# Start addresses of TensorE's tiles set to one place modulo 256 bytes

## The chip, the cores and the metric

The kernel runs on one core of one Trainium2 chip. The metric is the device time of one execution in microseconds (us); lower is better. TensorE multiplies (its weight loads are listed apart), VectorE (DVE) and ScalarE (ACT) do the elementwise work, GpSimd (POOL) does a little of it and issues some DMAs, and SyncE (SP) issues nearly all loads from memory.

## The reference, cut to what matters

Two layers over 256 latent tokens and 256 context tokens of width 1024, all in float32. In the last layer the context tokens only give keys and values, so that most products there have 256 columns (tokens) and not 512.

```
for l in range(DEPTH):                                  # DEPTH = 2
    h  = modulate(rmsnorm(x,  norm1_g[l]), sh1, sc1)    # latent tokens
    hc = modulate(rmsnorm(xc, norm1_g[l]), csh1, csc1)  # context tokens
    p  = h @ w_in[l]                                    # 1024 x 4608
    ...                                                 # conv branch, attention, gates
    x  = x + g1 * gated_merge(p[..., QKV_END:], y_conv, y_attn, w_out[l])
    h2 = modulate(rmsnorm(x, norm2_g[l]), sh2, sc2)
    x  = x + g2 * conv_ffn(h2, w_up[l], ffn_dw[l], ffn_dw_b[l], w_down[l])
    if not last: ...                                    # the same for xc
return rmsnorm(x, final_norm_g)
```

## The kernel before, in words

Activations are held transposed: a tile has 128 channels on the partitions and the tokens along the free axis, latent tokens in columns 0 to 255, context tokens in 256 to 511. Weights come from memory in units of 128 x 1024 float32 (512 KB), each of which holds eight 128 x 128 blocks.

To keep float32 accuracy at TensorE's fast rate for the type float32r, every operand is split into a high and a low part. A weight unit lands in `raw`; ACT copies it to `whi` (L167) and DVE subtracts to get `wlo` (L168); for 33 units the low part is made by a DMA that adds (`wadded`). `raw`, `whi` and `wlo` have four buffers each. Activations are split in the same way into pairs: `h[0][k]` and `h[1][k]` for k = 0 to 7, `oh`/`ol`, `sh`/`sl`, `fh`/`fl`.

`mm3` (L185 to L188) is the core of the program: one product of a weight block and an activation tile is three matmuls, L186 (whi, high), L187 (whi, low) and L188 (wlo, high). Before each of them TensorE loads the 128 x 128 weight block that it keeps, while the tokens of the matmul before are streamed. `group` (L190) is eight such triples over k into one bank. In the value projection (L723) the roles are changed: the block of `h` is kept, and 512 columns of `whi` or `wlo` are streamed.

The sequence of instructions on each engine is the order in which the program's generators are written out (`slot()`, the list `side`, the rates `pace` and `rate`), as far as buffers being free allow it. SP and POOL are in-order queues as well: a DMA that waits for its buffer holds back the DMAs behind it.

Where the tiles start matters for this change. In the built program, with addresses inside a partition taken modulo 256 bytes:

- Each `h` tile is 2 * S + 2 = 514 columns, that is 2056 bytes, and takes 2080. So the eight tiles `h[0][0]` to `h[0][7]` start at 0, 32, 64, 96, 128, 160, 192 and 224, and `h[1][k]` at the same place as `h[0][k]`.
- `whi` and `wlo` start at 0 (the four units that open the last layer's FFN, in a pool of their own, at 128). A block inside a unit is 512 bytes further on, so it has the same place.
- `fh`/`fl` start at 128 in both layers; `oh`/`ol`/`sh`/`sl` at 64 in layer 0 and at 128 in layer 1.

Below, the *difference* of a step is the start of the block being loaded minus the start of the tile being streamed, modulo 256. In a group over `h` it runs through 0, 224, 192, 160, 128, 96, 64, 32 as k goes from 0 to 7. In a group over `fh` it is 128 all the time.

The two extra columns of `h` serve one place: before the last layer's FFN, unnormalised activations are written into the context half of the tiles `z` (`plain`, L996) and a shift into the two columns behind them (`plain_shift`, L1002), and the first four up units multiply columns 256 to 513 of these tiles (`RAW`, 258 columns, L1091).

Of the kernel before, what the change touches and what calls it, by code (L numbers as in the profile page):

```python
# [30 lines left out]
MASKED = -1.0e30  # L31
UW = 1024
LAT, CTX = slice(0, S), slice(S, 2 * S)
ROWS = S // GW
# [19 lines left out]
def trunk(ctx: ExitStack, tc: tile.TileContext, xt, cvec, crow, wall, wada, params, bias_t, rope_t, out):  # L54
# [34 lines left out]
    def add_side(gen):  # L89
        side.append(gen)  # L90
# [86 lines left out]
    def wunit(l, u, at=None, cuts=1):  # L177
        w, more = wparts(l, u, at, cuts)
        more()
        return w  # L180
# [18 lines left out]

    def wadded(l, u):  # L200

        r = raw_unit(wall[l, u])
        hi = wp.tile([P, UW], F32R, tag="whi", bufs=4, name=nm("whi"))
        lo = wp.tile([P, UW], F32R, tag="wlo", bufs=4, name=nm("wlo"))
# [5 lines left out]
    def unit8(l, u, at=None):  # L210
        w = wadded(l, u) if (l, u) in ADDED else wunit(l, u, at)
        return [cols(w, i) for i in range(KD)]
# [405 lines left out]
    for l in range(DEPTH):  # L618
# [3 lines left out]
        ALL = slice(0, T)  # L622

        with ExitStack() if last else start as e1a:
            ea = e1a.enter_context(tc.tile_pool(name=f"ea{l}", bufs=1)) if last else ea0
# [74 lines left out]
            with ExitStack() as e1b:  # L700
# [27 lines left out]
                if l == 0:  # L728
# [14 lines left out]
                    rv = wp.tile([P, UW], F32, tag="raw", bufs=4, name=nm("raw"))  # L743
                    wv = [wp.tile([P, UW], F32R, tag=t, bufs=4, name=nm(t)) for t in ("whi", "wlo")]
# [3 lines left out]
                    wg = [wp.tile([P, UW], F32R, tag=t, bufs=4, name=nm(t)) for t in ("whi", "wlo")]  # L748
                    with tc.issue_after(lastev[0].ins):
# [63 lines left out]
                else:  # L813
                    sp.dma_start(rope, rope_t)
                    pg0 = [psum("sc") for _ in range(2)]
                    for uu in range(2):
                        wg = wunit(l, U_GLU0 + uu)
# [91 lines left out]
            with ExitStack() as e1c:  # L909
# [57 lines left out]
                def branch(base, xh, xl):  # L967
                    for n in range(0, KD, 2):
                        w = (wadded if (l, base + n // 2) in ADDED else wunit)(l, base + n // 2)
                        for i in range(2):  # L970
                            yield n + i, group(psum(), [cols(w, 4 * i + k) for k in range(KC)], xh, xl, ALL)
# [21 lines left out]

                RAW = slice(S, 2 * S + 2)

                def plain(k):  # L996
                    hi, lo = z[0][k][:, CTX], z[1][k][:, CTX]
                    g = gains[l, 4][:, k, 0:1]
                    lastev[0] = act.activation(hi, x[k][:, LAT], AF.Identity, scale=g)
                    dve.scalar_tensor_tensor(lo, x[k][:, LAT], g, hi.bitcast(F32), ALU.mult, ALU.subtract)  # L1000

                def plain_shift(k):  # L1002
                    hi, lo = (z[i][k][:, 2 * S : 2 * S + 2] for i in range(2))
                    b = mod(l, 3, k, 0).to_broadcast([P, 2])
                    act.copy(hi, b)
                    dve.tensor_tensor(lo, b, hi.bitcast(F32), ALU.subtract)
# [15 lines left out]
                pace[0] = 0.3  # L1022
                held = [unit8(l, U_WO + n) for n in range(NB, KD)]
                for s in range(NS if held else 0):
# [14 lines left out]
        with ExitStack() as e2:  # L1039
# [42 lines left out]
            ups = [U_UP + t for i in range(KF) for t in (i, KF + i)]  # L1082
            first = [unit8(l, u, ef if last else None) for u in ups[:4]]
            pss = [psum("sc"), psum("sc"), psum(), psum()]
            if last:
# [3 lines left out]
                for k in range(KD):  # L1089
                    for w, ps in zip(first, pss):  # L1090
                        mm3(ps[:, : S + 2], w[k], h2[0][k][:, RAW], h2[1][k][:, RAW], k == 0, k == KD - 1)  # L1091
# [44 lines left out]
            for i in range(2, KF):  # L1136
                w = [unit8(l, ups[2 * i + t]) for t in range(2)]
                pa, pg = (group(psum(), w_, *h2, ALL) for w_ in w)
# [9 lines left out]
            else:  # L1148
                pace[0] = 0.3
                row = lambda: ef.tile([P, UW], F32, tag="row", bufs=2, name=nm("row"))  # L1150
                add_side(ada_dots(1, range(40, 48), [across(ef, 0)], row))
            for streams, ns in [((0, 1), range(NB)), *(((s,), range(NB, KD)) for s in range(NS))]:
                wu = None
                c = slice(streams[0] * S, (streams[-1] + 1) * S)
                for n in ns:
                    ps = psum()
                    for k in range(KF):
                        t = n * KF + k
                        if t % 8 == 0 or not wu:
                            wu = wunit(l, U_DN + t // 8)  # L1160
                        mm3(ps[:, c], cols(wu, t % 8), fh[k][:, c], fl[k][:, c], k == 0, k == KF - 1)
# [163 lines left out]
```

## Time and profile before

| | before |
|---|---|
| time, median of 3 runs | 1105.96 us (1105.14 to 1106.23) |
| span of the profiled execution | 1105.0 us |
| TensorE busy | 1092.9 us (99%), 6886 matmuls |
| VectorE busy | 895.7 us (81%) |
| ScalarE busy | 567.9 us (51%) |
| read from memory | 187.63 MB, 171 GB/s over the span |
| granted TensorE clock | 0.997 |

The span runs from the first to the last instruction; the runs' median is 0.96 us above it, and that is taken as what lies around the span. A matmul's duration in the profile reaches past the start of the next one, so that durations overlap and add up to more than the span; what one matmul costs is the time from its start to the start of the next, which is called a *step* here. A count of matmuls in a window includes those that are already running at its edge (about two).

### The profile page before, as it was taken

The page shows a single profiled execution, that of the slowest core. Times are in us where ns is not written, and L with a number is a line of the kernel's source. Part 1 is how long each engine was busy: PE and PEld are TensorE (multiplying, and loading weights), DVE is VectorE, ACT ScalarE, POOL GpSimd, SP SyncE. Part 2 cuts the span into 40 slices and gives each one's busy share as a digit, 9 for nine tenths or more (in the row PEclk, how much of TensorE's full clock was granted, in tenths as well). Part 3 has the DMA queues.
Part 4 walks back from the last instruction along what each step waited for, and adds up shares of the span by engine and source line. Part 5 has one row for each costly group of instructions (what it writes and reads, how often), then busy time and mean ns, then how long its engine had stood idle before and what let it go on. Part 6 is the DMA issues. An engine that isn't in the chain of part 4 may idle for free.

```text
span 1105.0 us, 18022 instructions
## 1 busy us (share of the span) xinstructions
PE 1092.9 (99%) x6886; PEld 949.4 (86%) x6886; DVE 895.7 (81%) x1630; ACT 567.9 (51%) x943; POOL 43.5 (4%) x59
## 2 busy tenths in 40 slices
PE   9999999999999999999999999999999999999997
PEld 6777777788889888888888888998889999999997
DVE  5568898889998788888897555789799888988773
ACT  4458767445334534343434223444676667666642
POOL 1111110011000000000000000000000000000000
PEclk9999999999999999999999999999999999999998
DMA  9888664978843445445567666566644484666781
GB/s 364 287 226 225 143 167 103 290 241 218 259 134 115 129 142 168 150 155 153 172 189 232 207 190 177 182 205 190 192 133 138 153 283 145 202 191 182 228 259 56
DMA packets 59510, 209.26 MB, mean 189 GB/s; under 512 B 7200, under 2 KB 7456, under 8 KB 59424
## 3 DMA queue, kind: packets, MB, share of 16 engines
q1 hardware_dynamic: 54384, 190.77, 53.8%
q0 software_dynamic: 4752, 17.30, 8.2%
q8 instruction: 54, 0.88, 0.3%
q14 instruction: 32, 0.26, 0.1%
q10 hardware_dynamic: 288, 0.04, 0.0%
HBM read 187.63 MB, written 1.05 MB: 171 GB/s over the span
## 4 chain that ended last, share of the span: by engine, by line
PE 89%; DVE 3%; ACT 3%; DMA 2%; issue 1%; SPq 1%; DVEq 0%; ACTq 0%
PE main L186 26%; PE main L188 26%; PE main L187 26%; PE main L723 4%; DMA raw<-in_wall 1%; SPq L715 1%; PE sc L186 1%; PE sc L187 1%; PE sc L188 1%; PE po L219 1%; PE po L564 1%; DVE cb L659 1%; PE sc L481 1%; ACT whi L167 1%; DVE wlo L168 0%
## 5 line engine op out<-in xcount | busy, mean ns | idle before, releaser
L186 PE MATMUL main<-h,whi 128*128 128x256 f32 (+1 forms) x1328 | 447.4, 337 | 0.0
L188 PE MATMUL main<-h,wlo 128*128 128x256 f32 (+1 forms) x1328 | 443.4, 335 | 1.1 <-DVE wlo L168 1.1
L187 PE MATMUL main<-h,whi 128*128 128x256 f32 (+1 forms) x1328 | 442.5, 334 | 0.1
L167 ACT CAST whi<-raw 128x1024 fp32r<-128x1024 f32 (+1 forms) x211 | 217.8, 1036 | 239.8 <-DMA raw<-in_wall 116.3
L168 DVE TENSOR_TENSOR wlo<-raw,whi 128x1024 fp32r<-128x1024 f32 (+1 forms) x211 | 252.7, 1205 | 88.6 <-ACT whi L167 83.5
L186 PEld LDWEIGHTS main<-h,whi 128*128 128x128 f32 x1328 | 249.6, 188 | 30.4 <-issue 2.2
L188 PEld LDWEIGHTS main<-h,wlo 128*128 128x128 f32 x1328 | 249.4, 188 | 29.8 <-DVE wlo L168 1.5
L187 PEld LDWEIGHTS main<-h,whi 128*128 128x128 f32 x1328 | 249.9, 188 | 28.5 <-DVE h L391 0.5
L659 DVE SCALAR_TENSOR_TENSOR cb<-u,par,cb 128x512 f32<-128x512 f32 (+1 forms) x240 | 144.0, 615 | 2.8
L186 PE MATMUL main<-fh,whi 128*128 128x256 f32 (+1 forms) x386 | 123.0, 319 | 0.0
L187 PE MATMUL main<-fl,whi 128*128 128x256 f32 (+1 forms) x386 | 122.9, 319 | 0.0
L188 PE MATMUL main<-fh,wlo 128*128 128x256 f32 (+1 forms) x386 | 122.9, 318 | 0.0
L293 DVE CUSTOM_DVE_ANT_0 t<-raw,sb,par 128x1024 bf16<-128x1024 f32 x72 | 91.4, 1277 | 0.3 <-ACT sb L273 0.3
L187 PEld LDWEIGHTS main<-fl,whi 128*128 128x128 f32 x386 | 72.7, 188 | 5.6
L188 PEld LDWEIGHTS main<-fh,wlo 128*128 128x128 f32 x386 | 72.7, 188 | 5.6
L186 PEld LDWEIGHTS main<-fh,whi 128*128 128x128 f32 x386 | 72.7, 188 | 5.5
L1052 ACT ACTIVATE t<-main,par 128x512 f32<-128x512 f32 (+1 forms) x82 | 50.8, 669 | 38.5 <-PE main L188 38.5
L293 DVE CUSTOM_DVE_ANT_0 t<-own,sb,par 128x1024 bf16<-128x1024 f32 x48 | 60.3, 1278 | 1.9 <-DMA own<-in_wada 1.9
L205 ACT CAST whi<-raw 128x1024 fp32r<-128x1024 f32 x33 | 34.6, 1049 | 51.0 <-PE main L187 43.8
L1053 DVE SCALAR_TENSOR_TENSOR t<-main,par,t 128x510 f32<-128x510 f32 (+1 forms) x82 | 47.5, 614 | 10.2 <-ACT t L1052 9.8
L1056 DVE SCALAR_TENSOR_TENSOR t<-main,par,t 128x510 f32<-128x510 f32 (+1 forms) x82 | 46.6, 609 | 0.0
L390 ACT ACTIVATE h<-t,mod 128x256 fp32r<-128x256 f32 x56 | 25.2, 501 | 34.9 <-DVE t L389 34.7
(216 smaller groups left out, 1258.1 us busy)
## 6 DMA issues: line engine op xcount, KB each, us to landing
raw<-in_wall SPq DMA_DIRECT2D x240, 512.0 KB, 4.4
raw<-in_wada SPq DMA_DIRECT2D x64, 512.0 KB, 4.4
wlo<-raw POOLq DMA_DIRECT2D x33, 512.0 KB, 5.3
own<-in_wada SPq DMA_DIRECT2D x24, 512.0 KB, 5.5
bias<-in_bias_t SPq DMA_DIRECT2D x8, 520.0 KB, 5.3
row<-in_wada SPq DMA_DIRECT2D x8, 512.0 KB, 4.7
sb<-in_crow SPq DMA_DIRECT2D x5, 512.0 KB, 4.7
x<-in_xt SPq DMA_DIRECT2D x4, 512.0 KB, 5.2
```

The source lines that it names most:

```text
L167: act.copy(hi[:, c], r[:, c])
L168: dve.tensor_tensor(lo[:, c], r[:, c], hi[:, c].bitcast(F32), ALU.subtract)
L186: pe.matmul(ps, w[0], xh, start=start, stop=False)
L187: pe.matmul(ps, w[0], xl, start=False, stop=False)
L188: pe.matmul(ps, w[1], xh, start=False, stop=stop)
L205: act.copy(hi, r)
L293: dve.tensor_tensor_reduce(tmp().bitcast(BF16), r, v, 1.0, pr(l, BADA + n, 1), ALU.mult, ALU.add, mods[l][:, n, s : s + 1])
L659: dve.scalar_tensor_tensor(cb[j], src, w, cb[j], ALU.mult, ALU.add)
L723: mm = pe.matmul(pv[t], h1[n == 1][k][:, c], w[n == 2][:, b], start=k + n == 0, stop=k == KD - 1 and n == 2)
L1052: act.activation(c, pv_, AF.Identity, bias=pr(l, FDB + t, 1), scale=w[1])
L1053: dve.scalar_tensor_tensor(c[:, :, 1:], pv_[:, :, : S - 1], w[0], c[:, :, 1:], ALU.mult, ALU.add)
L1056: dve.scalar_tensor_tensor(c[:, :, : S - 1], pv_[:, :, 1:], w[2], c[:, :, : S - 1], ALU.mult, ALU.add)
```

## The change

Nothing is computed otherwise. Tiles are given other sizes and offsets, so that they start elsewhere:

- `h` tiles lose their two extra columns (2048 bytes). A filler tile and a wider `sil` shift what lies behind them. In the built program `h`, `fh`, `fl`, `oh`, `ol`, `sh` and `sl` then all start at 0 modulo 256.
- Weight tiles get 64 spare columns (4352 bytes, which is 17 * 256). A unit that is used with 512 columns starts at 0; one that is used with 256 columns (`narrow`) starts 16 columns, 64 bytes, further on. So the difference is 0 in every step of 512 columns and 64 in every step of 256 columns.
- The unnormalised activations get tiles of their own (`plains`, 264 columns each, starting at 0, 32, ... 224) instead of the context half of `z`. In the built program the shift can then be written earlier.
- The rows of the last modulation (`row`) take the buffers of `whi` in the FFN's own pool, which are four, instead of two of their own.

The diff, cut:

```diff
+NARROW = 16
+    fill = tp.tile([P, 32], F32, name="fill")
-    sil = ea0.tile([P, 2 * KD + 32], F32, name="sil")
+    sil = ea0.tile([P, 2 * KD + 48], F32, name="sil")
+    def weight_pair(narrow, at=None):
+        off = NARROW if narrow else 0
+        return [
+            (at or wp).tile([P, UW + 4 * NARROW], F32R, tag=t, bufs=4, name=nm(t))[:, off : off + UW] for t in ("whi", "wlo")
+        ]
-    def wparts(l, u, at=None, cuts=2):
+    def wparts(l, u, at=None, cuts=2, narrow=False):
         r = wp.tile([P, UW], F32, tag="raw", bufs=4, name=nm("raw"))
-        hi = (at or wp).tile([P, UW], F32R, tag="whi", bufs=4, name=nm("whi"))
-        lo = (at or wp).tile([P, UW], F32R, tag="wlo", bufs=4, name=nm("wlo"))
+        hi, lo = weight_pair(narrow, at)
...
     def h_tiles():
-        return [[hp.tile([P, 2 * S + 2], F32R, tag=f"h{i}{k}", name=nm("h")) for k in range(KD)] for i in range(2)]
+        return [[hp.tile([P, 2 * S], F32R, tag=f"h{i}{k}", name=nm("h")) for k in range(KD)] for i in range(2)]
...
+        if last:
+            rp = ctx.enter_context(tc.tile_pool(name="raws", bufs=1))
+            plains = [[rp.tile([P, S + 8], F32R, name=f"p{i}{k}") for k in range(KD)] for i in range(2)]
...
-                return group(psum(tag), unit8(l, U_IN + t), *h1, c)
+                return group(psum(tag), unit8(l, U_IN + t, c.stop == S), *h1, c)
...
-                    ps = group(psum(), unit8(l, U_WO + n), *z, ALL)
+                    ps = group(psum(), unit8(l, U_WO + n, last), *z, ALL)
...
-                w = [unit8(l, ups[2 * i + t]) for t in range(2)]
+                w = [unit8(l, ups[2 * i + t], last) for t in range(2)]
...
-                row = lambda: ef.tile([P, UW], F32, tag="row", bufs=2, name=nm("row"))
-                add_side(ada_dots(1, range(40, 48), [across(ef, 0)], row))
+                row = lambda: ef.tile([P, UW + 4 * NARROW], F32, tag="whi", bufs=4, name=nm("row"))[:, :UW]
+                add_side(ada_dots(1, range(40, 48), [across(ef, 0, tag="late")], row))
...
-                            wu = wunit(l, U_DN + t // 8)
+                            wu = wunit(l, U_DN + t // 8, narrow=len(streams) == 1)
```

The order of instructions on TensorE and POOL stays as it was. Two places move on the other engines.

On VectorE, at the end of layer 0, where the context tokens' sum of squares (`ss`) is closed and their norm (`red`) begins. Before:

```order
L168 TENSOR_TENSOR wlo_6699<-raw_6697,whi_6698 128x1024
L345 TENSOR_TENSOR ss_5533<-ss_5533,t_6558 128x256
L168 TENSOR_TENSOR wlo_6744<-raw_6742,whi_6743 128x1024
L367 TENSOR_SCALAR red_6658<-pt_6655 128x2
L168 TENSOR_TENSOR wlo_6786<-raw_6784,whi_6785 128x1024
```

And with the change:

```order
L352 TENSOR_TENSOR ss_5534<-ss_5534,t_6559 128x256
L1017 TENSOR_TENSOR p_6574<-mod_107,p_6566 128x2
L1017 TENSOR_TENSOR p_6575<-mod_107,p_6567 128x2
...
L1017 TENSOR_TENSOR p_6581<-mod_107,p_6573 128x2
L176 TENSOR_TENSOR wlo_6764<-raw_6762,whi_6763 128x1024
L374 TENSOR_SCALAR red_6678<-pt_6675 128x2
```

The eight subtractions of `plain_shift` (`p` is a tile of `plains`) came forward from the middle of layer 1; the eight small copies that feed them came forward on ScalarE in the same way.

On SyncE, in the last layer, where the up units of the FFN are loaded (`raw`) and the first rows of the last modulation (`row`) among them. Before:

```order
L164 DMA raw_9148<-in_wall 128x1024
L154 DMA row_10957<-in_wada 128x1024
L164 DMA raw_9154<-in_wall 128x1024
...
L164 DMA raw_9498<-in_wall 128x1024
L154 DMA row_11019<-in_wada 128x1024
L164 DMA raw_9582<-in_wall 128x1024
L164 DMA raw_9588<-in_wall 128x1024
L164 DMA raw_9658<-in_wall 128x1024
```

And with the change:

```order
L172 DMA raw_9602<-in_wall 128x1024
L172 DMA raw_9608<-in_wall 128x1024
L156 DMA row_10977<-in_wada 128x1024
L156 DMA row_11039<-in_wada 128x1024
L156 DMA row_11115<-in_wada 128x1024
L156 DMA row_11161<-in_wada 128x1024
L172 DMA raw_9678<-in_wall 128x1024
```

Two row loads moved back past the next up units, and two more came forward; the four stand together, behind the loads for the sixth pair of up units, and each waits for TensorE to give back a buffer of the FFN's first four units.

More of the change, by code (lines that the diff above doesn't have):

```diff
@@ L175, in wparts, with wunit @@
         return (hi, lo), more
-    def wunit(l, u, at=None, cuts=1):
-        w, more = wparts(l, u, at, cuts)
+    def wunit(l, u, at=None, cuts=1, narrow=False):
+        w, more = wparts(l, u, at, cuts, narrow)
         more()
@@ L198, in group, with wadded @@
         return ps
-    def wadded(l, u):
+    def wadded(l, u, narrow=False):
         r = raw_unit(wall[l, u])
-        hi = wp.tile([P, UW], F32R, tag="whi", bufs=4, name=nm("whi"))
-        lo = wp.tile([P, UW], F32R, tag="wlo", bufs=4, name=nm("wlo"))
+        hi, lo = weight_pair(narrow)
         act.copy(hi, r)
@@ L208, in wadded, with unit8 @@
         return hi, lo
-    def unit8(l, u, at=None):
-        w = wadded(l, u) if (l, u) in ADDED else wunit(l, u, at)
+    def unit8(l, u, narrow, at=None):
+        w = wadded(l, u, narrow) if (l, u) in ADDED else wunit(l, u, at, narrow=narrow)
         return [cols(w, i) for i in range(KD)]
@@ L743, in trunk @@
                     rv = wp.tile([P, UW], F32, tag="raw", bufs=4, name=nm("raw"))
-                    wv = [wp.tile([P, UW], F32R, tag=t, bufs=4, name=nm(t)) for t in ("whi", "wlo")]
+                    wv = weight_pair(False)
                     cuts = [slice(i * 512, (i + 1) * 512) for i in range(2)]
@@ L747, in trunk @@
                     rg = raw_unit(wall[l, U_GLU0])
-                    wg = [wp.tile([P, UW], F32R, tag=t, bufs=4, name=nm(t)) for t in ("whi", "wlo")]
+                    wg = weight_pair(False)
                     with tc.issue_after(lastev[0].ins):
@@ L968, in branch @@
                     for n in range(0, KD, 2):
-                        w = (wadded if (l, base + n // 2) in ADDED else wunit)(l, base + n // 2)
+                        w = (wadded if (l, base + n // 2) in ADDED else wunit)(l, base + n // 2, narrow=last)
                         for i in range(2):
@@ L992, in trunk @@
                 h2 = z
-                RAW = slice(S, 2 * S + 2)
+                RAW = slice(0, S + 2)
                 def plain(k):
-                    hi, lo = z[0][k][:, CTX], z[1][k][:, CTX]
+                    hi, lo = (plains[i][k][:, LAT] for i in range(2))
                     g = gains[l, 4][:, k, 0:1]
@@ L1002, in plain_shift @@
                 def plain_shift(k):
-                    hi, lo = (z[i][k][:, 2 * S : 2 * S + 2] for i in range(2))
+                    hi, lo = (plains[i][k][:, S : S + 2] for i in range(2))
                     b = mod(l, 3, k, 0).to_broadcast([P, 2])
@@ L1022, in trunk @@
                 pace[0] = 0.3
-                held = [unit8(l, U_WO + n) for n in range(NB, KD)]
+                held = [unit8(l, U_WO + n, True) for n in range(NB, KD)]
                 for s in range(NS if held else 0):
@@ L1082, in trunk @@
             ups = [U_UP + t for i in range(KF) for t in (i, KF + i)]
-            first = [unit8(l, u, ef if last else None) for u in ups[:4]]
+            first = [unit8(l, u, True, ef if last else None) for u in ups[:4]]
             pss = [psum("sc"), psum("sc"), psum(), psum()]
```

4 lines of the change are left out of this document (2 added, 2 removed).

## Prediction

> **What bounds the kernel now.** I read the page's shares and its chain first.
>
> ```profile
> PE 1092.9 (99%) x6886; PEld 949.4 (86%) x6886; DVE 895.7 (81%) x1630; ACT 567.9 (51%) x943; POOL 43.5 (4%) x59
> PE 89%; DVE 3%; ACT 3%; DMA 2%; issue 1%; SPq 1%; DVEq 0%; ACTq 0%
> ```
>
> TensorE is the bound: 89% of the chain that ended last. So the price is steps times the length of a step. The groups by line, different shapes apart (count | busy us, mean ns of one), give the counts; of three lines of one triple I show one:
>
> ```profile
> L186 PE MATMUL main<-h,whi 128*128 128x512 f32 x624 | 248.3, 398 | 0.0
> L186 PE MATMUL main<-h,whi 128*128 128x256 f32 x688 | 194.5, 283 | 0.0
> L186 PE MATMUL main<-fh,whi 128*128 128x256 f32 x260 | 73.2, 282 | 0.0
> L186 PE MATMUL main<-fh,whi 128*128 128x512 f32 x126 | 49.7, 395 | 0.0
> L723 PE MATMUL main<-whi,h 128*128 128x512 f32 x128 | 40.5, 401 | 0.1
> L723 PE MATMUL main<-wlo,h 128*128 128x512 f32 x64 | 24.9, 397 | 0.0
> L186 PE MATMUL sc<-h,whi 128*128 128x256 f32 x48 | 13.5, 281 | 0.0
> L186 PE MATMUL main<-oh,whi 128*128 128x512 f32 x32 | 12.4, 388 | 0.0
> L186 PE MATMUL main<-oh,whi 128*128 128x256 f32 x32 | 9.3, 290 | 0.0
> ```
>
> With 256 columns that is 3 x (688 + 260 + 48 + 32) + 96 = 3180 steps (96 for `sh`, like `oh`). With 512 columns at `h`, `fh` and L723 it is 3 x (624 + 126) + 192 = 2442, and at `oh` and `sh` 192.
>
> A step's length comes from stretches without waits. Busy time by window (us, PE, PEld, DVE, ACT):
>
> ```profile
> 945.00:1040.00 95.00, 95.00 (x805) 95.00 (x804) 80.62 (x134) 61.85 (x99) 0.00 (x0) 1.00 0.66 198
> 400.00:590.00 190.00, 190.00 (x819) 153.40 (x818) 163.09 (x240) 77.50 (x101) 0.00 (x0) 1.00 0.54 167
> 256.00:299.00 43.00, 43.00 (x190) 35.27 (x189) 39.31 (x63) 18.41 (x22) 4.34 (x5) 1.00 0.91 260
> ```
>
> Less two for the edges, 256 columns take 95 us / 803 = 118.3 ns, 512 columns over `h` 190 / 817 = 232.6 ns, and over `oh` and `sh` 43 / 188 = 228.7 ns. The same work has two lengths, at a granted clock of 1.00 in all three rows. What differs is where tiles start: the difference is 192 throughout in the third window, and runs through all eight values in the second. The groups inside these windows say how long a matmul lasts in each:
>
> ```profile
> L187 PE MATMUL main<-h,whi 128*128 128x512 f32 x273 | 107.3, 393 | 0.0
> L187 PE MATMUL main<-h,whi 128*128 128x256 f32 x249 | 69.7, 280 | 0.0
> L187 PE MATMUL main<-ol,whi 128*128 128x512 f32 x32 | 12.5, 392 | 0.0
> ```
>
> Over the three lines the means are 394.7, 280.7 and 391.3 ns, so a step is the duration less 162.3 in each. With that the duration of a single matmul can be read as a step.
>
> **The 256-column steps (difference 64).** Before, 64 comes up at k = 6 of a group over `h`. Where layer 0 multiplies its first up units for the context tokens, six steps in a row have it. Matmuls in order of time (start us, us):
>
> ```profile
> 361.14 0.28 PE L186 MATMUL sc<-h,whi 128*128 128x256 f32 x1
> ...
> 361.85 0.28 PE L186 MATMUL sc<-h,whi 128*128 128x256 f32 x1
> 361.97 0.28 PE L187 MATMUL sc<-h,whi 128*128 128x256 f32 x1
> ...
> 362.54 0.28 PE L186 MATMUL sc<-h,whi 128*128 128x256 f32 x1
> ```
>
> From 361.14 to 361.85 (difference 96) six steps take 0.71 us, 118 ns each. From 361.97 to 362.54 (difference 64) five take 0.57 us, 114 each. In the middle of that stretch, 362.26 to 362.40, and at the same k for the latent tokens, 355.75 to 355.90, one row of each (the others of the triple read the same):
>
> ```profile
> L186 PE MATMUL sc<-h,whi 128*128 128x256 f32 x1 | 0.3, 276 | 0.0
> ...
> L187 PE MATMUL sc<-h,whi 128*128 128x256 f32 x1 | 0.3, 281 | 0.0
> ```
>
> 276 ns is a step of 113.7, and it repeats: a settled state. But 281 at the same difference is not it:
>
> ```profile
> 355.46 0.28 PE L186 MATMUL sc<-h,whi 128*128 128x256 f32 x1
> ...
> 356.52 0.28 PE L186 MATMUL sc<-h,whi 128*128 128x256 f32 x1
> ```
>
> Nine steps in 1.06 us, 117.8 each. So a step depends on the difference and on the state in which it is entered, and at 64 there are two states. Bounds: 113.7 and 117.8. With one difference throughout, TensorE has long to settle; I count 85 steps in 100 in the short state: 114.3. Saved: (118.3 - 114.3) x 3180 = 12.7 us; bounds 14.6 and 1.6.
>
> **The 512-column steps (difference 0).** Difference 0 is k = 0 of a group over `h`: three steps, from 430.26 on. Two narrow windows give their durations in order, first L186 and L187, then L187 and L188:
>
> ```profile
> L186 PE MATMUL main<-h,whi 128*128 128x512 f32 x1 | 0.4, 397 | 0.0
> L187 PE MATMUL main<-h,whi 128*128 128x512 f32 x1 | 0.4, 392 | 0.0
> ...
> L188 PE MATMUL main<-h,wlo 128*128 128x512 f32 x1 | 0.4, 393 | 0.0
> ```
>
> 397, 392, 393 are steps of 234.7, 229.7 and 230.7. The first follows a change of difference; the mean of all is 231.7, of the last two 230.2. Nothing longer shows difference 0, so the bounds are 228.7, the best constant difference seen, and 234.7; I take 230.9, between the two means. Saved: (232.6 - 230.9) x 2442 = 4.2 us. `oh` and `sh` of layer 0 lose their better place: (230.9 - 228.7) x 192 = 0.4 us.
>
> **What moves.** The eight copies and subtractions of the shift:
>
> ```profile
> L1005 ACT CAST h<-mod x8: 183/193/194, 856.0 to 858.8; 128x2 fp32r<-128x2 f32 x8
> L1006 DVE TENSOR_TENSOR h<-mod,h x8: 151/152/154, 857.4 to 869.2; 128x2 fp32r<-128x2 f32 x8
> 722.68 0.16 DVE L367 TENSOR_SCALAR red<-pt 128x2 f32<-128x2 f32 x1
> ```
>
> On DVE 8 x 0.152 = 1.2 us now stand ahead of `red` at 722.68, on ACT 8 x 0.193 = 1.5 us ahead of a weight copy. Queued behind are the context norm and one weight split. Layer 1 starts with products of latent tokens alone, which hide the norm; the split feeds TensorE with up to four buffers in hand. Uncovered it would be 1.5 us; I take 0.2. In the middle of layer 1 DVE is rid of 1.2 us.
>
> The four row loads (`row`):
>
> ```profile
> 895.28 0.43 SPq L154 DMA_DIRECT2D row<-in_wada  x1
> 910.06 0.42 SPq L154 DMA_DIRECT2D row<-in_wada  x1
> 920.00:945.00 25.00, 24.43 (x201) 23.82 (x201) 23.63 (x52) 20.82 (x41) 0.00 (x0) 1.00 0.32 94
> ```
>
> Each now waits until the first up units are multiplied. Behind them on SP is `raw` for the seventh pair, which cannot be issued before TensorE has gone on to the third pair anyway, since `raw` and `whi` have four buffers. It is needed eight groups of 24 steps later, 22 us. Four loads of 512 KB are 2.1 MB; at the 198 GB/s of the stretch after it, 10.6 us, and DMA runs at a third (0.32) there. Hidden: 0; without the cover a few us.
>
> **What takes some back.** Where another engine is full, TensorE cannot go faster:
>
> ```profile
> 800.00:820.00 20.00, 20.00 (x174) 17.90 (x173) 19.84 (x60) 15.16 (x38) 0.00 (x0) 1.00 0.50 152
> 820.00:840.00 20.00, 20.00 (x225) 18.59 (x224) 19.39 (x41) 17.50 (x38) 1.59 (x1) 1.00 0.39 120
> ```
>
> DVE has 39.2 of 40 us. At most 399 steps there, x 4.0 = 1.6 us, are lost; I take 1.5 for this and the waits around it.
>
> **Sum.** -12.7 - 4.2 + 0.4 + 0.2 + 1.5 = -14.8 us on the span of 1105.0, which makes 1090.2. The median of the runs, 1105.96, is 0.96 above that span, and with it the forecast is 1091 us.
>
> **A rule against it.** In the Trainium skill, page "TensorE: Matmul & The Clock Gate", section "Part 2: What happens when you issue a matmul", the streamed operand and the weight load have independent read ports, and loading the next tile's weights doesn't take read bandwidth from the running matmul. By that rule no start address matters and the time stays. The rows at k = 6 disagree.
>
> **Rivals.**
> - *No effect* (0.08): step lengths come from something else that goes with k, as other engines' accesses. Against it: 276 repeats and the pattern of a group does too. 1106.
> - *The short state is not kept* (0.12): 117.8 with 256 columns, 231.7 with 512. -1.6 - 2.2 + 0.6: 1102.8. For it: 355.46 to 356.52.
> - *Others take it back* (0.08): between 720 and 945 in layer 1 DVE and ACT pace the work, and of its 225 us / 118.3 = 1900 steps none gets shorter: 7.6 us less gain, 1099. For it: the two rows of 800 to 840; against it: DVE has 80.62 of 95 us from 945 on.
> - *Slower: a constant difference locks into a long state* (0.05). Difference 0 with 256 columns, around 345.8, shows one:
>
> ```profile
> L188 PE MATMUL sc<-h,wlo 128*128 128x256 f32 x1 | 0.3, 283 | 0.0
> 345.35 0.28 PE L186 MATMUL sc<-h,whi 128*128 128x256 f32 x1
> 345.95 0.28 PE L186 MATMUL main<-h,whi 128*128 128x256 f32 x1
> ```
>
>   Five steps of 120. If 64 did that, +1.7 x 3180 = 5.4; with 512 columns at 234.7, +2.1 x 2442 = 5.1, and 1.2 at `oh` and `sh`: 1117.7. It decides once the mean step passes 118.3 or 232.6.
> - *All excess over streaming goes* (0.03): a fixed difference removes every collision of load and stream. By rows, each step is then at most the shortest one read, 113.7 and 228.7: -14.6 - 9.5, 1081.9 or less. For it: 113.7 is shorter than any mean here; against it: no 512-column step at difference 0 comes near 228.7. The Trainium skill, same page, section "Back-to-back issue gap", gives N / 2.4 + 2.5 ns for a step, 109.2 and 215.8, with which the time would be near 1032; no run here shows such a step.
>
> **How the numbers follow.** The forecast has 0.64. Its own range: 256 columns all short (-14.6), 512 at 228.7 (-9.5) and nothing taken back give 1082; a third of the steps long and no gain with 512 columns give 1098. The range goes on to the state that is not kept, and a little beyond either end: 1081 to 1103. It leaves out no effect, the slower case and the lowest one, 16 in 100. A measurement of this kernel tells about 0.2%, 2.2 us, from no change. Faster: 0.64 + 0.12 + 0.08 + 0.03, less 0.01 for a short gain that is lost = 0.86; same 0.09; slower 0.05.
>
> **What would show it.** In windows of up units and down units of layer 1 some 835 matmuls in 95 us where 803 were, durations near 276; in 400 to 590 of layer 0 durations near 393 on all three lines, where they are 396, 393 and 395. L1006 before `red` at the end of layer 0, and TensorE not waiting for `h` there. Four row loads at one time near 920 and no idle TensorE behind them. If durations don't move, the first rival holds; if they are 281 with 256 columns, the second; if they fall but the time doesn't, the third. The prediction is wrong in its mechanism if the two kinds of steps differ from 276 and 393 in the long stretches, and wrong in its size alone if they do so by a few ns with the time following.

## The result, and the profile after

The changed kernel takes **1089.2 us** (median of 5 executions, 1084.03 to 1090.1), the kernel before beside it 1105.3 us: a ratio of 0.9843, 95% interval [0.9824, 0.9862]. The forecast was 1091. The profiled execution of the change is the one of 1084.03 us, with a span of 1082.3. Executions of the change lie at two times, near 1084 and near 1089; the experiments below say why. One execution of a kernel below (all weights at 0) took 2165.03 us, about twice its others; it is left out, and its cause is not known. Lines have moved by 7 to 11: L194 to L196 are the three matmuls of a triple, L176 is the split, L734 the value projection.

The page of the changed kernel, busy time by engine and the chain by engine:

```profile
PE 1067.4 (99%) x6886; PEld 936.8 (87%) x6886; DVE 892.9 (83%) x1630; ACT 567.7 (52%) x943; POOL 43.5 (4%) x59
PE 86%; DVE 8%; ACT 3%; SPq 1%; issue 1%; DMA 1%; DVEq 0%; ACTq 0%
```

TensorE is still the bound. Its busy time fell by 25.5 us (1092.9 to 1067.4) with the same 6886 matmuls, and its idle time rose by 2.8 (from 1105.0 - 1092.9 = 12.1 to 1082.3 - 1067.4 = 14.9). The span fell by the difference, 22.7. In the chain that ended last, VectorE's share went from 3% to 8%.

The groups by line, shapes apart, of the changed kernel; the columns are count, busy us and mean ns of one:

```profile
L194 PE MATMUL main<-h,whi 128*128 128x512 f32 x624 | 244.7, 392 | 0.0
L194 PE MATMUL main<-h,whi 128*128 128x256 f32 x688 | 191.7, 279 | 0.2 <-DVE qk L877 0.2
L194 PE MATMUL main<-fh,whi 128*128 128x256 f32 x260 | 72.1, 277 | 0.0
L194 PE MATMUL main<-fh,whi 128*128 128x512 f32 x126 | 49.0, 389 | 0.0
L734 PE MATMUL main<-whi,h 128*128 128x512 f32 x128 | 40.0, 398 | 0.1
L194 PE MATMUL main<-oh,whi 128*128 128x512 f32 x32 | 12.4, 389 | 0.0
```

The groups over `h` and `fh` and the value projection are shorter, with 512 columns by 6 ns (398 to 392 over `h`, 395 to 389 over `fh`); this line over `oh` is not (388 to 389), though the mean of its triple is (391.3 to 389). The windows of the prediction, of the changed kernel (us from the start; the window's length, PE busy with the count of matmuls, then PEld, DVE, ACT, POOL, clock, DMA share, GB/s):

```profile
945.00:1040.00 95.00, 95.00 (x841) 95.00 (x840) 81.77 (x134) 62.60 (x97) 0.00 (x0) 1.00 0.70 217
400.00:590.00 190.00, 190.00 (x840) 157.30 (x840) 166.70 (x246) 80.55 (x104) 0.00 (x0) 1.00 0.55 172
```

Less two for the edges, a step is 95 us / 839 = 113.2 ns (118.3 before) and 190 / 838 = 226.7 (232.6 before), at the same clock. The groups inside these two windows, and between 252 and 295 us (`oh`, `sh` of layer 0), one of three equal lines each:

```profile
L194 PE MATMUL main<-h,whi 128*128 128x256 f32 x202 | 55.8, 276 | 0.0
...
L195 PE MATMUL main<-h,whi 128*128 128x512 f32 x268 | 104.3, 389 | 0.0
...
L194 PE MATMUL main<-oh,whi 128*128 128x512 f32 x32 | 12.4, 389 | 0.0
```

276 ns is what the prediction had read at k = 6; 389 is less than any of its means over a triple, the 391.3 over `oh` and `sh` among them.

From the start times of all matmuls, steps without a wait: 512 columns 232.28 to 227.06 ns (some 2640 of them, -13.8 us), 256 columns 118.40 to 114.64 (some 3250, -12.2 us), all the rest +3.3 us. That is the -22.7 of this execution.

### The profile page after: what moved, and what is told of

Same layout as the page of the kernel before. It is cut to its first block, busy times and chain, and to the rows that moved or that the text cites. A ratio compares the mean times of both kernels' runs of the same rounds, so it can differ in the third digit from the quotient of the medians.

```text
span 1082.3 us, 18018 instructions
## 1 busy us (share of the span) xinstructions
PE 1067.4 (99%) x6886; PEld 936.8 (87%) x6886; DVE 892.9 (83%) x1630; ACT 567.7 (52%) x943; POOL 43.5 (4%) x59
## 4 chain that ended last, share of the span: by engine, by line
PE 86%; DVE 8%; ACT 3%; SPq 1%; issue 1%; DMA 1%; DVEq 0%; ACTq 0%
PE main L194 25%; PE main L196 25%; PE main L195 25%; PE main L734 4%; DVE cb L670 2%; SPq L726 1%; DVE wlo L176 1%; PE sc L194 1%; PE sc L195 1%; PE sc L196 1%; PE po L226 1%; PE po L571 1%; DMA raw<-in_wall 1%; PE sc L488 0%; DVE qk L877 0%
## 5 line engine op out<-in xcount | busy, mean ns | idle before, releaser
L194 PE MATMUL main<-h,whi 128*128 128x256 f32 (+1 forms) x1312 | 436.4, 333 | 0.2 <-DVE qk L877 0.2
L196 PE MATMUL main<-h,wlo 128*128 128x256 f32 (+1 forms) x1312 | 433.1, 331 | 2.0 <-DVE wlo L176 2.0
L195 PE MATMUL main<-h,whi 128*128 128x256 f32 (+1 forms) x1312 | 433.6, 331 | 0.1
L176 DVE TENSOR_TENSOR wlo<-raw,whi 128x1024 fp32r<-128x1024 f32 (+1 forms) x211 | 252.7, 1205 | 82.5 <-ACT whi L175 79.5
L194 PEld LDWEIGHTS main<-h,whi 128*128 128x128 f32 x1312 | 246.3, 188 | 28.1 <-issue 2.9
L196 PEld LDWEIGHTS main<-h,wlo 128*128 128x128 f32 x1312 | 246.0, 188 | 27.3 <-DVE wlo L176 2.6
L195 PEld LDWEIGHTS main<-h,whi 128*128 128x128 f32 x1312 | 246.6, 188 | 24.8 <-DVE h L398 0.5
L194 PE MATMUL main<-fh,whi 128*128 128x256 f32 (+1 forms) x386 | 121.1, 314 | 0.0
L196 PE MATMUL main<-fh,wlo 128*128 128x256 f32 (+1 forms) x386 | 121.0, 314 | 0.0
L194 PEld LDWEIGHTS main<-fh,whi 128*128 128x128 f32 x386 | 72.4, 188 | 4.9
L196 PEld LDWEIGHTS main<-fh,wlo 128*128 128x128 f32 x386 | 72.5, 188 | 4.9
```

Of the source, the lines that this page charges most:

```text
L194: pe.matmul(ps, w[0], xh, start=start, stop=False)
L195: pe.matmul(ps, w[0], xl, start=False, stop=False)
L196: pe.matmul(ps, w[1], xh, start=False, stop=stop)
```

## The experiments

One theory stood first, **difference and state**: a step depends on the difference, and at 64 also on a state that is entered and kept. The rivals were **waits** (steps as long as the other engines leave them), **boundary** (only the place of the streamed tile counts) and **other edits** (the moved rows and shifts bring the gain).

### The same kernel again

There is no edit.

> The changed kernel once more, with nothing altered, for a second profile. Theory 'difference and state' (a step's length is set by the difference between the start of the block being loaded and the tile being streamed, and with 256 columns at difference 64 by one of two states): times spread over 1084 to 1090 us again; 512-column steps are 226.7 ns in every stretch, and what differs between a fast and a slower execution is how many 256-column steps sit at 116 to 118 ns and not at 113.3: a time of 1089 has at least one of the long stretches of layer 1 (about 840 steps of up units, 530 of down units) in the longer state. Rival 'waits' (the spread comes from DMA and from waits on other engines): step lengths are the same in both profiles and the time between the stretches differs.

Measured: 1086.83 us median, executions at 1083.95, 1084.79, 1088.87 and 1089.11; ratio 0.9822 [0.9799, 0.9846]. The profiled one is the execution of 1088.87. Its two windows:

```profile
945.00:1040.00 95.00, 95.00 (x809) 95.00 (x808) 78.38 (x127) 60.11 (x94) 0.00 (x0) 1.00 0.67 202
400.00:590.00 190.00, 190.00 (x840) 157.34 (x839) 167.24 (x247) 80.27 (x104) 0.00 (x0) 1.00 0.54 172
```

and its largest group in the first:

```profile
L196 PE MATMUL main<-h,wlo 128*128 128x256 f32 x202 | 56.8, 281 | 0.0
```

The same program has 809 matmuls where the other execution has 841, and 281 ns where that has 276: 95 / 807 = 117.7 ns. The 512-column window is the same. So the two times of the kernel go with two lengths, or states, of the 256-column steps. The last stretch without a wait (1264 steps, from 930 us to 1073 or 1078) is at 113.3 in one execution and at 117.8 in the other, from its first steps to its last; 1264 x 4.45 ns = 5.6 us, a little more than the 4.8 us between the two spans (1082.3 and 1087.1); other stretches and waits make up the rest. Shorter stretches show the same: after the first few steps the length does not change within a stretch of one difference, and most are at one of the two.

### All weights at 0

```diff
-        off = NARROW if narrow else 0
+        off = 0
```

> Weights of 256-column units start at 0 too, not 64 bytes further on; all else as in the changed kernel. 'Difference and state': 512-column steps stay at 226.7 ns, 256-column steps (3180) go to 120 ns as before at difference 0, which is 5.4 ns more than the 114.6 of the changed kernel's profile: about 17 us more than the changed kernel, 1105 us or so. Rival 'boundary' (what counts is that the streamed tile begins on a 256-byte boundary, whatever the weights do): 256-column steps stay near 114.6, 1089 us. Rival 'other edits' (the separate tiles, the moved loads and the order): 1089 us.

Measured: 1097.24 us (1097.24 to 1097.32, 3 executions), ratio 0.9918 [0.9898, 0.9938]. Its windows:

```profile
945.00:1040.00 95.00, 95.00 (x794) 95.00 (x793) 77.75 (x129) 60.08 (x94) 0.00 (x0) 1.00 0.64 197
400.00:590.00 190.00, 190.00 (x840) 157.39 (x839) 166.96 (x246) 80.30 (x105) 0.00 (x0) 1.00 0.55 170
```

With difference 0, 256 columns take 95 / 792 = 120.0 ns, and in every stretch: one state only. That is longer than before the change. 512 columns are untouched. The forecast of the theory was too high, since it set the steps of 120 against 114.6 as the usual mean; against the 116.6 of the repeated execution it is (120.0 - 116.6) x 3250 = 11 us, and 10.4 were measured. The rivals boundary and other edits, by which nothing should change, fall: the only edit is 64 bytes of place in the weights.

### All weights at 64

```diff
-        off = NARROW if narrow else 0
+        off = NARROW
```

> Weights of all units start at 64, those used with 512 columns too. 'Difference and state': 256-column steps as in the changed kernel; 512-column steps (2490) go from 226.7 to 233.3 ns, the length that the value projection shows before the change at difference 64: 16 us more than the changed kernel, about 1105 us. Rival 'boundary': 226.7 ns and 1089 us. Rival 'other edits': 1089 us.

Measured: 1102.24 us (1101.23 to 1102.71), ratio 0.9962 [0.9947, 0.9977]. Its windows:

```profile
945.00:1040.00 95.00, 95.00 (x809) 95.00 (x809) 80.63 (x136) 63.25 (x101) 0.00 (x0) 1.00 0.65 199
400.00:590.00 190.00, 190.00 (x816) 153.10 (x815) 163.10 (x239) 77.18 (x101) 0.00 (x0) 1.00 0.53 166
```

512 columns at difference 64 take 190 / 814 = 233.4 ns, more than before the change. 6.7 ns x 2640 = 17.7 us, of which 15.4 show in the time. This and the run above reject waits as well: the same engines do the same work, and the step follows the place. With the weights moves also the place that ScalarE and VectorE write them to; that a step stays the same through 1264 steps while those engines start and stop speaks against such writes as the cause, but no run moves them apart. The Trainium skill, page "TensorE: Matmul & The Clock Gate", section "Part 2: What happens when you issue a matmul", lets the next weight load take no read bandwidth from the running matmul; read as the prediction read it, that no start address matters, it would make the two runs equal to the change. They differ from it, and from each other by 5 us, so the measurement decides against that reading. Whether it is read bandwidth that is lost, no run here shows.

### The tiles of `h` stepped again, all else as changed

```diff
-        return [[hp.tile([P, 2 * S], F32R, tag=f"h{i}{k}", name=nm("h")) for k in range(KD)] for i in range(2)]
+        return [[hp.tile([P, 2 * S + 8], F32R, tag=f"h{i}{k}", name=nm("h")) for k in range(KD)] for i in range(2)]
...
```

All weights start at 0 as well, without the spare columns (not shown). The moved rows and the moved shift stay as in the change.

> All weights at 0 and the h tiles 2080 bytes apart again, so that their difference runs through 0, 224, ... 32 as before the change; fh, fl, oh, ol, sh and sl stay at 0, and the separate tiles, the moved loads and the order stay as changed. 'Difference and state': steps over h back to 232.5 and 118.4 ns; fh and oh with 512 columns at 226.7 (588 steps, together some 3 us less than before), with 256 columns at 120 (some 970 steps, 1.5 us more): 1104 us. 'Other edits': 1089 us. 'Boundary': k = 0 alone is short, about 1103 us.

Measured: 1104.14 us (1103.59 to 1104.86, 10 executions), ratio 0.9981 [0.9972, 0.9991]. Its windows:

```profile
945.00:1040.00 95.00, 95.00 (x804) 95.00 (x804) 80.30 (x137) 62.72 (x100) 0.00 (x0) 1.00 0.65 198
400.00:590.00 190.00, 190.00 (x818) 153.41 (x818) 162.81 (x240) 78.05 (x101) 0.00 (x0) 1.00 0.53 168
```

804 and 818 stand beside 805 and 819 of before. With the eight differences back, the gain is gone. Together the other edits are worth at most the 2 us that are left. Of these, 1.5 were expected from `fh`, `oh` and `sh`, whose difference is still 0 here (shorter steps with 512 columns, longer ones with 256).

### Every tile 128 bytes further on

```diff
+    cp.tile([P, 32], F32, name="plus")
```

> The change with a filler of 128 bytes a partition ahead of all pools, so that every tile that TensorE streams or keeps lies 128 bytes further on; the differences stay at 0 (512 columns) and 64 (256 columns). Difference theory: only the difference counts; steps 226.7 and a mixture of 113.3 and 117.8, time 1084 to 1090, as the change. Rival, place: the place of the streamed tile within 256 bytes counts too (before, fh lay at 128); 512 columns between 228 and 233, time 1092 to 1102.

Measured: 1084.97 us, executions at 1084.65, 1084.88, 1085.07 and 1088.61; ratio 0.9816 [0.98, 0.9832]. The profiled execution is that of 1088.61:

```profile
945.00:1040.00 95.00, 95.00 (x809) 95.00 (x809) 78.60 (x127) 60.33 (x95) 0.00 (x0) 1.00 0.67 204
400.00:590.00 190.00, 190.00 (x840) 157.34 (x839) 166.40 (x245) 79.85 (x104) 0.00 (x0) 1.00 0.54 172
```

The two times and the two counts are those of the repeat. A shift of all tiles together changes nothing that shows, so it is the difference that counts, at least for a shift of 128 bytes.

### Other differences with 256 columns: 48, 80, 192

```diff
-        off = NARROW if narrow else 0
+        off = 12 if narrow else 0      (48 bytes; 20 for 80 bytes, 48 for 192 bytes)
```

> The change with the weights of 256-column units 48 bytes further on and not 64, so that their difference is 48; 512 columns as in the change. Difference theory: the step lies between those at 0 (120) and at 64 (113.3 or 117.8), so 113 to 120; if 48 lies nearer to a good place than 64, all stretches are short and the time is 1081 to 1084; if 64 is a place of its own, 118 to 120 and 1093 to 1097. Rival, waits (the steps adapt to what the other engines give): the time does not move, 1084 to 1090.

> As the one with 48, with 80 bytes for 256 columns: between the steps at 64 (113.3 or 117.8) and at 96 (118, as before the change). Difference theory: 113 to 118; 1081 to 1084 if only the short step is left, 1090 to 1093 if only the long one is. Rival, waits: 1084 to 1090.

> The change with weights of 256-column units at 192 instead of 64 bytes, 512 columns as in the change: the last of the four multiples of 64 that is not measured with 256 columns (120 at 0, 113.3 or 117.8 at 64, near 118.7 at 128). Theory: a step of its own between 113 and 120 and kept in every stretch, or two states again; single steps before the change had 119.1 at this difference, so 1093 to 1097 is the likeliest, 1084 to 1089 the other bound.

Measured: 48 bytes 1101.35 us (1094.2 to 1102.14, 6 executions), ratio 0.9932 [0.9905, 0.9959]; 80 bytes 1094.64 (1094.24 to 1096.36), 0.9899 [0.9884, 0.9914]; 192 bytes 1091.58 (1091.28 to 1091.97), 0.9872 [0.9858, 0.9885]. The first window of each, first 48:

```profile
945.00:1040.00 95.00, 95.00 (x772) 95.00 (x772) 76.91 (x128) 59.51 (x94) 0.00 (x0) 1.00 0.61 187
```

then 80:

```profile
945.00:1040.00 95.00, 95.00 (x802) 95.00 (x802) 78.83 (x132) 60.91 (x97) 0.00 (x0) 1.00 0.65 199
```

then 192:

```profile
945.00:1040.00 95.00, 95.00 (x809) 95.00 (x808) 79.43 (x131) 61.29 (x96) 0.00 (x0) 1.00 0.65 201
```

Steps of 123.4, 118.8 and 117.7 ns. With 48 there are three states: stretches at 117.8, at 118.3 and at 123.3, and the executions again lie at two times (1094.2 and 1094.8; 1101.1 to 1102.1). The last stretch, 1290 steps, was at 123.3 in the profiled execution of 1102.14; 1290 x 5.5 ns = 7.1 us lies between the two times. With 80 there is one state. With 192 the two states of 64 come back, 117.8 in nearly all stretches and 113.3 in three short ones. My expectation that a neighbour of 64 might have the short state alone is wrong, and what I held likeliest for 192 (1093 to 1097) was too long: of the places run, 64 and 192 are the good ones, 64 the better.

### 512 columns at 240

```diff
-        off = NARROW if narrow else 0
+        off = NARROW if narrow else 60
```

> The change with weights of 512-column units at 240 instead of 0, so that the difference of 512-column steps is 240 (in the value projection, where the roles are changed, 16); 256 columns as in the change. Measured so far: 226.7 at 0, 228.9 at 192, 233.3 at 64. Difference theory: 226 to 229, time from 2 us below the change to 5 us above it (1082 to 1094). If 0 is a place of its own, as with rivals that see only whether tiles start on a multiple of 256 bytes: 232 or more, 1098 or more.

Measured: 1090.5 us (1085.76 to 1093.21, 4 executions), ratio 0.9854 [0.9828, 0.988]. The window of layer 0's up units:

```profile
400.00:590.00 190.00, 190.00 (x840) 157.37 (x839) 166.47 (x245) 79.59 (x103) 0.00 (x0) 1.00 0.53 170
```

and the value projection, whose difference is 16 here, in the groups by line:

```profile
L734 PE MATMUL main<-whi,h 128*128 128x512 f32 x128 | 41.0, 405 | 0.1
```

At 240 the step in this window is the same 226.7 as at 0; in the value projection, at 16, a matmul lasts 405 ns where it lasts 398 at 0. So 0 is not the only good place, but nothing better turned up.

### Setting the state by a step aside: 96, 0, and 0 then 96

If the state at 64 is chosen at its entry, what stands ahead should matter. Two profiles from above bear on that. In the change, 256-column steps (difference 64) follow 512-column steps (difference 0) without a wait at 318.21, 671.59, 742.95 and 751.24 us, and all four stretches are long from their first step. With all weights at 64 the same four places follow other differences (64, and 192 in the value projection), and all four settle in the short state. Windows inside the stretch of 153 steps, first of the change, then with all weights at 64:

```profile
673.00:689.00 16.00, 16.00 (x138) 16.00 (x137) 10.76 (x15) 7.52 (x10) 0.00 (x0) 1.00 0.76 238
...
686.00:702.00 16.00, 16.00 (x143) 16.00 (x143) 11.24 (x15) 8.15 (x11) 0.00 (x0) 1.00 0.77 242
```

Then a few units at another difference should set the state. Six of the weight units used with 256 columns are moved, each at the head of a stretch (the last at 937 us):

```diff
+    units = [0]
...
-        off = NARROW if narrow else 0
+        units[0] += narrow
+        off = 0 if not narrow else 24 if units[0] - 1 in {1, 9, 28, 59, 71, 80} else NARROW
```

24 columns are 96 bytes. The second kernel has 0 in place of 24. In the third the last of the six is one unit later, and the unit ahead of it, at 937 us, is at 0.

> The change, with six weight units of 256 columns (one at the head of a stretch in layer 0's up units, at 672, 754, 876, 911 and 937 us) at 96 instead of 64 bytes; all others as in the change. Before the change a step from difference 96 to 64 led to 117, 116, 114 and then 113.3 in most places. Theory (the state at difference 64 is chosen by how it is entered, and kept): behind each such unit the steps are 113.3 in every execution, also in the last stretch of 1200 steps, so that the executions no longer lie at two times; 1082 to 1085, all within 2 us; the six units themselves cost 6 x 24 x 4.6 ns = 0.7 us. Rival (the state follows from what other engines do in the stretch): 113.3 and 117.8 stay mixed behind these units, and executions lie at 1084 and at 1089 as before.

> As the one with six units at 96, with these units at 0 (settled step 120, a regular pattern). Theory: what follows is again the same in every execution, since the entry into 64 is always the same one; whether it is the short or the long state is not known ahead, so 1083 to 1086 or 1089 to 1093, and nothing in between. Rival (other engines): a mixture of 1084 and 1089.

> As the kernel with six units at 96, but the last of them is at 940 us and the unit ahead of it, at 937 us, is at 0, so that the difference at the head of the last long stretch goes 64, 0, 96, 64. Behind units at 0 the state was the same everywhere (long), so 0 should wipe out what was before, and the entry from 96 into 64 is then always the same one. Theory (state chosen by the entry): the last stretch is the same in every execution: short, 1081.5 to 1082.5 with the other stretches short too (up to 1085 where some are long), which is likelier since 96 led to short in most places; or long in all of them, 1087 to 1089. Rival (a part of it is chance in every entry from 96): one execution in five near 1088.5, as without the unit at 0.

Measured: at 96, 1081.92 us, executions at 1081.79, 1081.83, 1081.92, 1084.88 and 1088.59, ratio 0.9801 [0.978, 0.9822]; at 0, 1089.51 (1088.92 to 1090.02, 4 executions), 0.9853 [0.9838, 0.9868]; 0 then 96, **1082.66 (1082.47 to 1083.64, 5 executions), 0.9789 [0.9776, 0.9802]**.

Groups in narrow windows (lines are shifted by three), at 96: from 931 to 934 us, ahead of the last unit, and from 941 to 944, behind it:

```profile
L199 PE MATMUL main<-h,wlo 128*128 128x256 f32 x10 | 2.6, 281 | 0.0
...
L199 PE MATMUL main<-h,wlo 128*128 128x256 f32 x10 | 2.8, 276 | 0.0
```

The stretch entered long, and 24 steps at 96 made it short, with no wait in between. From the start times, the stretch behind each of the six units is short in this execution (113.3 or 113.4), with four of them long before (117.8) and two short; the steps at 96 themselves are 117.4 behind a long stretch and 120.0 behind a short one. (The first unit is used a second time, at 332 us, where a wait cuts it in two; behind that the steps are long.) At 0, from 941 to 944:

```profile
L197 PE MATMUL main<-h,whi 128*128 128x256 f32 x10 | 2.8, 281 | 0.0
```

and the long window:

```profile
945.00:1040.00 95.00, 95.00 (x809) 95.00 (x809) 78.41 (x128) 60.09 (x93) 0.00 (x0) 1.00 0.66 202
```

Behind all six units at 0 the steps are 117.8, also at 875 and 910 us, where they were 113.4 and 113.5 ahead of the unit; all four executions are within 1.1 us. The third kernel, 0 then 96, in the long window:

```profile
945.00:1040.00 95.00, 95.00 (x841) 95.00 (x840) 80.12 (x131) 61.94 (x96) 0.00 (x0) 1.00 0.70 218
```

All five of its executions are within 1.2 us, and each is below every execution of the change (the lowest were 1083.95 and 1084.03). One execution of each kernel is profiled; that the others had the same states is read from their times alone. So what stands ahead of a stretch chooses its state, and the rival by which other engines choose it falls: between these kernels the other engines' work is the same. The expectation for 96 alone, all executions within 2 us, failed: two of five stayed above 1084, so this entry alone does not settle it. They weren't profiled, so which of their stretches were long isn't shown.

## Why the prediction was right, and where it was not

The time was forecast at 1091 and came out at 1089.2, with the range and the sign right. The mechanism holds too: steps follow the difference. But two terms were off in opposite directions, and the sum is nearer than its parts by luck. By the prediction's own signs the two sizes are what was wrong: 389 ns where it had 393, and in part of the executions 281 where it had 276. Against the profiled executions at both times (us):

| term | predicted | execution of 1084.0 | execution of 1088.9 |
|---|---|---|---|
| 256 columns, difference 64 | -12.7 | -12.2 | -5.8 |
| 512 columns, `oh` and `sh` among them | -3.8 | -13.8 | -13.8 |
| moved shift, rows, taken back by others | +1.7 | +3.3 | +1.7 |
| span | -14.8 | -22.7 | -17.9 |

**The 512-column step was mis-sized.** The step that failed is "Nothing longer shows difference 0, so the bounds are 228.7, the best constant difference seen, and 234.7". Three steps behind a change of difference are no settled stretch: from 234.7, 229.7 and 230.7 I took 230.9, while the settled step is 226.7, below both bounds. The lower bound, 228.7, was the step at another difference (192), and there was no reason why 0 should not lie below it. The same choice made `oh` and `sh` lose 0.4 us; they gained (391 to 389 ns, means of the triple). The lowest rival came nearest on this term with -9.5, priced at 228.7; what was held against it, that no 512-column step at difference 0 comes near 228.7, did not hold. That all collisions of load and stream are gone, as it had it, isn't shown.

**With 256 columns the two states were right, their share was not.** 276 and 281 are what the long windows show. "With one difference throughout, TensorE has long to settle; I count 85 steps in 100 in the short state" failed: the state does not settle with time, it is kept until the next wait or change of difference, as the stretch of 1264 steps shows in both executions. From the means of 114.64 and 116.63, taken as mixtures of 113.3 and 117.8, an estimate of (117.8 - 114.64) / 4.45 = 71 in 100 were short in one execution and (117.8 - 116.63) / 4.45 = 26 in the other. So the rival *the short state is not kept* (117.8) holds for the longest stretch of many executions: six of the nine of the change and its repeat lie near 1089, and the one of them that was profiled has it there. What saved the forecast from it is the 512-column term.

**The slower rival** named a real thing: difference 0 with 256 columns is a long state of 120 ns and the only one there. At 64 the long state is 117.8, still a little below the 118.4 of before, so it could not make the kernel slower.

**What others take back** came out larger in one execution, and at another place. What TensorE waited for over the whole span, before (us in total, times, longest):

```profile
PE main L188 <- DVE wlo L168: 1.1, 2, 0.6
...
PE sc L481 <- ACT pT L553: 0.4, 1, 0.4
```

and with the change:

```profile
PE main L196 <- DVE wlo L176: 2.0, 2, 1.3
...
PE sc L488 <- ACT pT L560: 0.9, 1, 0.9
...
PE sc L488 <- DVE qk L877: 0.6, 1, 0.6
...
PE pt L366 <- DVE ss L352: 0.5, 1, 0.5
```

The prediction placed it between 800 and 840 us. It came in layer 0's attention (the products of L488 there wait 1.9 us for ScalarE and VectorE, 0.6 before) and in one wait of 1.3 us for a weight split for a matmul at 926.65 us. That matmul in the order of time (start us, us):

```profile
926.65 0.38 PE L196 MATMUL main<-h,wlo 128*128 128x256 f32 x1 [1.29 <-DVE wlo L176]
```

and the window around it:

```profile
925.00:930.00 5.00, 3.71 (x32) 3.50 (x31) 5.00 (x11) 2.68 (x5) 0.00 (x0) 1.00 0.38 105
```

VectorE is busy for all 5.00 us, so the split stood behind its other work: TensorE has caught up with VectorE, as the third rival had it, for 1.3 us instead of 7.6.

**The moved parts cost nothing that shows.** The subtractions of the shift, of the changed kernel, by line, then `red`, the row loads, and the window behind them:

```profile
L1017 DVE TENSOR_TENSOR p<-mod,p x8: 153/153/153, 709.1 to 709.6; 128x2 fp32r<-128x2 f32 x8
```

```profile
L374 DVE TENSOR_SCALAR red<-pt x1: 152/152/152, 710.8 to 710.8; 128x2 f32<-128x2 f32 x1
```

```profile
L156 SPq DMA_DIRECT2D row<-in_wada x4: 328/426/430, 900.8 to 902.1; - x4
```

```profile
910.00:925.00 15.00, 15.00 (x135) 15.00 (x134) 14.16 (x32) 13.87 (x27) 0.00 (x0) 1.00 0.49 141
```

The eight stand ahead of `red` as foreseen, but start over 0.5 us, not 1.2: instructions of 152 ns overlap, and adding their durations was too much. The only wait of TensorE near there is the 0.5 us for `ss`, whose last sum stands ahead of the eight in the order (708.75 us on VectorE). The four row loads are issued in one go, and from 910 to 925 TensorE is busy all the time.

The formula of the Trainium skill (page "TensorE: Matmul & The Clock Gate", section "Back-to-back issue gap") is given there for a single matmul apart, with no allowance for a weight load; 109.2 and 215.8 ns are the estimates by it for 256 and 512 columns. The shortest settled steps of all runs here, each with a weight load, are 113.3 and 226.7, so even the best places stay 4 and 5% above it.

## What to carry to other kernels

Where TensorE is the bound and loads a new weight block for each matmul, take the start of the loaded block minus the start of the streamed tile, modulo 256 bytes, as a size to be tuned for each number of columns apart, and hold it constant over the whole stage; here it was worth 1.6%, and 2.1% with the units at 0 and 96 added. Read a settled step only from a stretch long enough to repeat: three steps behind a change say neither its size nor its bounds. When equal executions lie at two times, compare the counts of matmuls in one long window of each before any other cause is sought, and try a few steps at another difference at the head of that stretch.

## What was not expected of the hardware

Settled steps by difference, float32r, from the stretches of the runs above (ns):

| difference | 256 columns | 512 columns |
|---|---|---|
| 0 | 120.0 | 226.7 |
| 48 | 117.8, 118.3 or 123.3 | not run |
| 64 | 113.3 or 117.8 | 233.3 |
| 80 | 118.7 | not run |
| 96 | 117.4 or 120.0 (24 steps at a time) | not run |
| 128 | 118.7 (before, `fh`) | 232.4 (before, `fh`) |
| 192 | 113.3 or 117.8 | 228.7 (before, `oh` and `sh`) |
| 240 | not run | 226.7 |

- The best places for 512 columns are 0 and 240; 0 is among the worst for 256 columns (120.0), and 64, the best for 256, is the worst of those run for 512 (233.3).
- The steps at 0 and 64 are multiples of 6.67 ns, or such and two thirds: 17 (113.3), 17 2/3 (117.8), 18 (120.0), 34 (226.7), 35 (233.3). What this unit is, no run here says.
- At some differences (48, 64, 192) two or three step lengths exist, and each lasts for up to 1290 steps in a row. Entering 64 from 0 without a wait gave the long one in every case read, from 96 the short one in all but one, where a wait fell between. What in the entry decides is open, and so is why the 96 alone failed in two of five executions.
- Why the difference sets the step is not shown by any run. The period of 256 bytes is not varied by itself either: 0 and 128 differ (226.7 and 232.4 with 512 columns), so it is not 128, and all of a kind's weight buffers, 4352 = 17 x 256 bytes each, show one step within a stretch, which speaks for 256 and not 512 if they lie one behind the other.
